# TensorE order written out at three hand-overs of a one-layer trunk: first-token products between transposes, out projection by token halves

## The chip, the cores and the metric

The kernel runs on one core of one Trainium2 chip. The metric is the device time of one execution in microseconds. A core has five engines with an instruction queue each, and each queue runs in order: PE (TensorE, the matrix products), DVE (VectorE), ACT (ScalarE), POOL (GpSimd) and SP (SyncE, which here only starts DMA transfers).

## The reference

One layer over 1024 tokens and 1024 channels, all float32:

```
x = x + 0.5 * (silu(n1 @ w_gate) * (n1 @ w_up)) @ w_down     n1 = rmsnorm(x)        ("f1")
h = rmsnorm(x);  [u v | q k val | gate logits] = h @ w_in                            (mixer)
yA = u * (W_s layernorm(v) + b)       yB = stick-breaking attention, 16 heads of 64
x = x + (sigmoid(gA) * (yA @ W_A) + sigmoid(gB) * (yB @ W_B)) @ W_out
x = x + 0.5 * swiglu(rmsnorm(x))                                                     ("f2")
y = rmsnorm(x)
```

The hidden width of the two feed-forward blocks is 2816.

## The kernel before

**Products.** Every float32 operand is split into a high part (ACT casts it to fp32r) and the rest (a subtraction on DVE or POOL), and one product is three matmuls, high x high, high x low and low x high. Tokens come as eight tiles of 128 (t0 to t7); t0 to t3 are the low half, t4 to t7 the high half.

**A feed-forward block** (`ffn`) multiplies 2x2 block matrices with seven products in place of eight. `right_forms` prepares the token side: for each tile it loads x, takes the sum of squares on ACT (L105), the power -1/2 on POOL (L109), multiplies by the gain on DVE (L123, two halves of 512 channels), transposes eight 128x128 blocks on PE (L204, `nt`) and writes the result by `put` (L208 to L212). A low tile fills the forms B11 and B21, and POOL adds their two parts into `keep` (L218). A high tile makes T2, T1, T3, T4 and B22 from sums with `keep` (L222 to L231); the low parts of T1, T3 and T4 are POOL's. The heart of a high tile is this:

```
tt(t1, n[0], keep[0, t - 4], op=ALU.subtract)
tt(t2, n[1], t1, op=ALU.subtract)
put("T2", t2, tt)
put("T1", t1, pt)
tt(t3, n[1], b12, op=ALU.subtract)
put("T3", t3, pt)
```

Behind the preparation stand the *heads* of the first four weight columns (L269: 24 matmuls of 512 columns each, with B11 and B21, so with low tokens alone), then for each of 22 columns a *tail* (L289: five products with T2, T1, T3, T4 and B22). The down projection ends with a phase called `last` (L398 to L417), in which each finished pair of tiles is written to DRAM, normed and transposed (`after`, `norm_t`, L143) for the mixer.

**The mixer** starts with the value projection `proj_v` (tile `pv`, L67 to L69). It ends with the out projection: `down` takes a fourth of the contraction at a time, for all eight tiles and two column halves: 64 pieces `pd` of six matmuls of 512 columns. In the last fourth each finished tile goes to DRAM (`xres`, L743), and f2 loads it from there (`xr`, L188).

**Order.** Outside of what a program writes by hand, a scheduler with its own timing model orders each engine's queue. In the kernel before it orders everything. It put all 64 transposes of a preparation in front of the heads, and 32 transposes between the last product of f1 and the first of the mixer.

Of the kernel before, what the change touches and what calls it, by code (L numbers as in the profile page):

```python
# [23 lines left out]
XNB = 5  # L24
# [8 lines left out]
class Kernel:  # L33
# [3 lines left out]
    def __init__(self, ctx, tc, a, out):  # L37
        self.tc, self.nc, self.a, self.out, self.ctx = tc, tc.nc, a, out, ctx
        pool = lambda name, bufs, **k: ctx.enter_context(tc.tile_pool(name=name, bufs=bufs, **k))
        self.dram = pool("dram", 1, space=bass.MemoryType.DRAM)  # L40
        self.const = pool("const", 1)
        self.hp = pool("hp", 4)

# [5 lines left out]
    def load_w(self, src, a, b, early=False):  # L49

        nc = self.nc
        raw = self.wp.tile([P, 1024], F32, tag="raw", bufs=2, name="raw")
        nc.sync.dma_start(out=raw.rearrange("p (a b) -> p a b", a=a), in_=src)
        wr = self.wp.tile([P, 2, 1024], F32R, tag="wr", bufs=3, name="wr")
        nc.scalar.copy(wr[:, 0, :], raw)  # L55
        (nc.gpsimd if early else nc.vector).tensor_tensor(wr[:, 1, :], raw, wr[:, 0, :].bitcast(F32), op=ALU.subtract)  # L56
        v = wr.rearrange("p t (a b) -> p t a b", a=a)
        return v[:, 0], v[:, 1]
# [41 lines left out]
    def rstd(self, x2):  # L100
        nc = self.nc
        ss = self.np_.tile([P, 2], F32, tag="ss", name="ss")
        sq = self.psum("p3", "sq")
        for i in range(2):
            nc.scalar.activation(sq, x2[i], AF.Square, accum_out=ss[:, i:i + 1])  # L105
        r = self.np_.tile([P, 2], F32, tag="rs", name="rs")
# [5 lines left out]
    def normed(self, x, gain, tiles, offload):  # L112
# [5 lines left out]
        r = self.rstd(x)  # L118
# [15 lines left out]
    def norm_t(self, x, t, gain, h, offload=1):  # L134

        nc = self.nc
        half, c = t // 4, (t % 4) * P
        xns = [self.np_.tile([P, HALF], F32, tag="xn", bufs=XNB, name="xn") for _ in range(2)]
        self.normed(x[t], gain, xns, offload)
        for i, xn in enumerate(xns):  # L140
            ps = self.psum("p2", "nt")
            for k in range(4):
                nc.tensor.transpose(ps[:, k * P:(k + 1) * P], xn[:, k * P:(k + 1) * P], self.ident)  # L143
            o = [h[half][part][:, i * 4:i * 4 + 4, c:c + P] for part in range(2)]
            self.split(o[0], o[1], ps.rearrange("p (k c) -> p k c", k=4))
# [7 lines left out]
    def form(self, pool, tag, bufs, src):  # L153

        f = pool.tile([P, 2, HALF], F32R, tag=tag, bufs=bufs, name=tag)
        self.split(f[:, 0, :], f[:, 1, :], src)
        return f
# [17 lines left out]
    def right_forms(self, xsrc, gain_src, tp):  # L175


        nc, tt, pt = self.nc, self.nc.vector.tensor_tensor, self.nc.gpsimd.tensor_tensor
        names = ("B11", "B21", "T2", "T1", "T3", "T4", "B22")
        T = {n: (self.hp if i < 4 else tp).tile([P, 4, 2, HALF], F32R, tag="h", name=n) for i, n in enumerate(names)}  # L180
        with self.tc.tile_pool(name="pre", bufs=1, reuse_waits="tile") as pre:
            tmp = lambda tag, bufs: pre.tile([P, HALF], F32, tag=tag, bufs=bufs, name=tag)
            self.np_ = pre
            gain = pre.tile([P, D], F32, tag="gain", name="gain")

            def load(t):
                x = pre.tile([P, D], F32, tag="xr", bufs=2, name="xr")
                nc.sync.dma_start(out=x, in_=xsrc[t * P:(t + 1) * P, :])  # L188
                return x

            keep = {}
            nxt = load(0)
            nc.sync.dma_start(out=gain, in_=gain_src.partition_broadcast(P))
            cut = lambda y: [y[:, i * HALF:(i + 1) * HALF] for i in range(2)]
            r3 = lambda y: y.rearrange("p (k c) -> p k c", k=4)
            for t in range(NT):
                x, nxt = nxt, load(t + 1) if t + 1 < NT else None
                xn = [tmp("xn", 4) for _ in range(2)]
                self.normed(cut(x), cut(gain), xn, 0)
                n = []  # L200
                for i in range(2):
                    ps = self.psum("ps", "nt")
                    for k in range(4):
                        nc.tensor.transpose(ps[:, k * P:(k + 1) * P], xn[i][:, k * P:(k + 1) * P], self.ident)  # L204
                    n.append(ps)
                c = (t % 4) * P

                def put(name, src, sub):  # L208
                    hi, lo = T[name][:, :, 0, c:c + P], T[name][:, :, 1, c:c + P]
                    nc.scalar.copy(hi, r3(src))  # L210
                    sub(lo, r3(src), hi.bitcast(F32), op=ALU.subtract)
                    return hi.bitcast(F32), lo.bitcast(F32)  # L212

                if t < 4:
                    for i, name in enumerate(("B11", "B21")):
                        hi, lo = put(name, n[i], tt)
                        keep[i, t] = tmp("keep", 8)
                        pt(r3(keep[i, t]), hi, lo, op=ALU.add)  # L218
                else:
                    t1, t2, t3, t4 = (tmp("t", 4) for _ in range(4))  # L220
                    b12 = tmp("b12", 1)
                    tt(t1, n[0], keep[0, t - 4], op=ALU.subtract)  # L222
                    nc.scalar.copy(b12, n[0])
                    tt(t2, n[1], t1, op=ALU.subtract)
                    put("T2", t2, tt)
                    put("T1", t1, pt)
                    tt(t3, n[1], b12, op=ALU.subtract)
                    put("T3", t3, pt)
                    put("B22", n[1], tt)
                    tt(t4, t2, keep[1, t - 4], op=ALU.subtract)  # L230
                    put("T4", t4, pt)  # L231
        return T

    def ffn(self, xsrc, gain_src, wg, wu, wd, before, after):

        nc, tc, tt = self.nc, self.tc, self.nc.vector.tensor_tensor
        nff, nj, nhead = DFF // P, DFF // P // 2, 4

# [7 lines left out]
        with ExitStack() as outer:  # L246
# [3 lines left out]
            rawt = lambda: bp.tile([P, D], F32, tag="raw", bufs=4, name="raw")  # L250


            with tc.tile_pool(name="tp", bufs=3, reuse_waits="tile") as tp:
                T = self.right_forms(xsrc, gain_src, tp)
                with tc.tile_pool(name="pa", bufs=1, reuse_waits="tile") as pa:
                    tile = lambda tag, bufs: pa.tile([P, HALF], F32, tag=tag, bufs=bufs, name=tag)

                    def weights(w, f):
                        r = rawt()
                        nc.sync.dma_start(out=r.rearrange("p (k c) -> p k c", k=NK), in_=w[:, f * P:(f + 1) * P].rearrange("(k p) c -> p k c", p=P))  # L260
                        return cut(r)

                    def product(ps, src, right, first, last=True):
                        f = self.form(bp, "wf", 8, src)
                        for k in range(4):
                            ks = slice(k * P, (k + 1) * P)
                            self.mm3f(ps, f[:, 0, ks], f[:, 1, ks], T[right][:, k, 0, :], T[right][:, k, 1, :], first and k == 0, last and k == 3)

                    def head(f):  # L269

                        gate = weights(wg, f)
                        b, a = self.psum("ps", "pb"), self.psum("ps", "pa")
                        product(b, gate[0], "B11", True)
                        p1 = tile("pe", 3)
                        nc.scalar.copy(p1, b)
                        product(a, gate[1], "B21", True)
                        glo = tile("gs", 6)
                        tt(glo, a, p1, op=ALU.add)
                        return gate, b, glo

                    def gated(g, u):

                        s = tile("gs", 6)
# [5 lines left out]
                    def tail(f, gate, b, glo):  # L289
# [18 lines left out]
                        ghi = tile("gs", 6)  # L308
                        tt(ghi, d, w, op=ALU.add)
                        return lo, gated(ghi, uhi)  # L310
# [26 lines left out]
                    heads = {f: head(f) for f in range(nhead)}  # L337
                    for f in range(nff):
                        out = tail(f, *(heads.pop(f) if f in heads else head(f)))
# [7 lines left out]
            with tc.tile_pool(name="pb", bufs=1, reuse_waits="tile") as pb:  # L347
# [11 lines left out]
                def pform(j, src):  # L359
                    return self.form(bp, "wf", 8, src) if j % 2 == 0 else self.form(pb, "pf", 8, src)  # L360
# [36 lines left out]

                def last(js, ts, load=True):  # L398
                    for j in js:
                        if load:  # L400
                            fs[j] = [pform(j, y) for y in pair([dst("a22t4", j)])]
# [3 lines left out]
                last(range(3), range(4))  # L405
                for t in range(4):
                    tt(xh(t + 4, 0), old[t], xh(t + 4, 0), op=ALU.add)
                    tt(xh(t + 4, 1), old[t], xh(t + 4, 1), op=ALU.add)
                after(0, cut(x[0]), cut(gain), 2)
                after(1, cut(x[1]), cut(gain), 2)  # L410
# [366 lines left out]
```

## Time and profile before

| | |
|---|---|
| median of three runs | 2587.96 us (2587.29 to 2589.17) |
| the profiled execution | 2589.35 us, its span 2587.6 us |
| PE busy | 2442.4 us of the span (94%) |
| DVE, ACT, POOL busy | 1715.2, 1048.5, 367.1 us |
| mean granted TensorE clock | 0.975 |

The page of the profile divides the span into 40 slices of 64.7 us and gives each a digit, the busy share in tenths. All DMA of the kernel goes through SP's one queue (313.58 MB). Times in the views are microseconds from the start of the span.

### The profile page before, as it was taken

The numbers are of one execution on the slowest core, as the hardware profiler recorded it, in microseconds if no ns is written. First come the engines' busy times: TensorE is split into PE (matmuls) and PEld (weight loads), VectorE is DVE, ScalarE is ACT, GpSimd is POOL, SyncE is SP. The second block draws the span as 40 slices with busy tenths as digits, with TensorE's granted clock in tenths as the row PEclk, the third lists the DMA queues.
The fourth block names the chain that finished last, engine by engine and source line by source line (L and its number), as shares of the span: only waits on it lengthen the run. The fifth ranks groups of instructions, "written<-read, shape, count | busy, mean of one in ns | idle before, by whom it ended". The sixth has DMA issues, their size and how long they took to land.

```text
span 2587.6 us, 33119 instructions
## 1 busy us (share of the span) xinstructions
PE 2442.4 (94%) x12140; PEld 2069.8 (80%) x12140; DVE 1715.2 (66%) x2617; ACT 1048.5 (41%) x1988; POOL 367.1 (14%) x518
## 2 busy tenths in 40 slices
PE   2999999999999999999999999999929999999998
PEld 2888888788788888888888888888718888887887
DVE  7777777565638878887665555145577777775655
ACT  4333333344536666666422222221043333333535
POOL 4000000000214454444300000000040000000002
PEclk9999999999999999999999999999959999999999
DMA  4345535775421212122111122123243555356754
GB/s 138 116 169 176 171 128 173 250 271 187 139 74 40 58 42 58 42 59 56 34 49 55 46 70 66 55 71 107 87 133 110 171 179 169 129 171 245 263 188 138
DMA packets 250882, 315.69 MB, mean 122 GB/s; under 512 B 14816, under 2 KB 172000, under 8 KB 250720
## 3 DMA queue, kind: packets, MB, share of 16 engines
q1 hardware_dynamic: 250720, 313.58, 37.5%
q8 instruction: 95, 1.56, 0.3%
q14 instruction: 67, 0.55, 0.1%
HBM read 224.93 MB, written 80.22 MB: 118 GB/s over the span
## 4 chain that ended last, share of the span: by engine, by line
PE 58%; DVE 2%; ACT 1%; issue 1%; POOL 1%; DMA 1%; SPq 0%; POOLq 0%; DVEq 0%; ACTq 0%
PE pj L67 6%; PE pj L69 6%; PE pj L68 6%; PE pd L172 4%; PE pd L173 4%; PE pd L171 4%; PE pb L171 2%; PE pb L172 2%; PE pb L173 2%; PE av L532 2%; PE pv L68 2%; PE pv L69 2%; PE pv L67 2%; PE tr L525 2%; PE pa L68 1%; PE pa L67 1%
## 5 line engine op out<-in xcount | busy, mean ns | idle before, releaser
L73 ACT CAST wf<-raw 128x512 fp32r<-128x512 f32 x276 | 164.7, 621 | 301.0 <-PE pd L173 105.0
L74 DVE TENSOR_TENSOR wf<-raw,wf 128x512 fp32r<-128x512 f32 x276 | 183.9, 688 | 142.8 <-ACT wf L73 142.7
L67 PE MATMUL pj<-h,wr 128*128 128x512 f32 x640 | 253.0, 395 | 8.0 <-DVE q L74 8.0
L68 PE MATMUL pj<-h,wr 128*128 128x512 f32 x640 | 251.7, 393 | 0.0
L69 PE MATMUL pj<-h,wr 128*128 128x512 f32 x640 | 251.4, 393 | 0.1
L508 DVE TENSOR_TENSOR_SCAN kp<-kp 128x128 f32<-128x128 f32 (+7 forms) x128 | 181.5, 1423 | 46.5 <-POOL kp L506 45.1
L73 ACT CAST wf<-ws 128x512 fp32r<-128x512 f32 x176 | 108.4, 623 | 195.3 <-PE pd L173 126.6
L56 DVE TENSOR_TENSOR wr<-raw,wr 128x1024 fp32r<-128x1024 f32 x80 | 98.0, 1225 | 82.8 <-ACT wr L55 82.6
L512 POOL TENSOR_TENSOR bt<-bt,kp 128x512 f32<-128x512 f32 (+4 forms) x128 | 132.4, 1035 | 123.3 <-DVE kp L508 97.7
L67 PE MATMUL pv<-wr,h 128*128 128x256 f32 x512 | 146.7, 288 | 1.9 <-ACT vg L574 1.9
L68 PE MATMUL pv<-wr,h 128*128 128x256 f32 x512 | 146.2, 286 | 0.9 <-DVE wr L56 0.9
L67 PEld LDWEIGHTS pj<-h,wr 128*128 128x128 f32 x640 | 121.1, 189 | 32.3 <-DVE q L74 8.6
L69 PE MATMUL pv<-wr,h 128*128 128x256 f32 x512 | 146.2, 286 | 0.0
L69 PEld LDWEIGHTS pj<-h,wr 128*128 128x128 f32 x640 | 121.0, 189 | 25.2 <-DVE wr L56 0.3
L68 PEld LDWEIGHTS pj<-h,wr 128*128 128x128 f32 x640 | 121.0, 189 | 23.6
L55 ACT CAST wr<-raw 128x1024 fp32r<-128x1024 f32 x80 | 84.1, 1052 | 130.9 <-PE pd L69 53.6
L171 PE MATMUL pb<-T,wf 128*128 128x512 f32 x352 | 136.9, 389 | 0.0
L172 PE MATMUL pb<-T,wf 128*128 128x512 f32 x352 | 136.9, 389 | 0.0
L173 PE MATMUL pb<-T,wf 128*128 128x512 f32 x352 | 136.9, 389 | 0.0
L74 DVE TENSOR_TENSOR wf<-ws,wf 128x512 fp32r<-128x512 f32 x176 | 120.0, 687 | 24.7 <-ACT wf L73 24.4
L172 PE MATMUL pd<-wf 128*128 128x512 f32 x336 | 131.4, 391 | 0.0
L173 PE MATMUL pd<-wf 128*128 128x512 f32 x336 | 131.0, 391 | 0.0
(210 smaller groups left out, 6505.7 us busy)
## 6 DMA issues: line engine op xcount, KB each, us to landing
raw<-in_ff_w_down_dram SPq DMA_DIRECT2D x66, 512.0 KB, 6.0
raw<-in_w_in_dram SPq DMA_DIRECT2D x56, 512.0 KB, 3.9
raw<-in_ff_w_gate_dram SPq DMA_DIRECT2D x52, 512.0 KB, 4.3
raw<-in_ff_w_up_dram SPq DMA_DIRECT2D x44, 512.0 KB, 4.7
f_t2t<-as SPq DMA_DIRECT2D x22, 512.0 KB, 4.1
f_a11a<-act SPq DMA_DIRECT2D x44, 256.0 KB, 3.9
f_s2s<-as SPq DMA_DIRECT2D x22, 512.0 KB, 2.8
f_s3s<-as SPq DMA_DIRECT2D x22, 512.0 KB, 5.6
```

The source lines that it names most:

```text
L55: nc.scalar.copy(wr[:, 0, :], raw)
L56: (nc.gpsimd if early else nc.vector).tensor_tensor(wr[:, 1, :], raw, wr[:, 0, :].bitcast(F32), op=ALU.subtract)
L67: mm(ps, lhsT=lh, rhs=rh, start=first, stop=False)
L68: mm(ps, lhsT=lh, rhs=rl, start=False, stop=False)
L69: mm(ps, lhsT=ll, rhs=rh, start=False, stop=last)
L73: self.nc.scalar.copy(hi, src)
L74: self.nc.vector.tensor_tensor(lo, src, hi.bitcast(F32), op=ALU.subtract)
L171: mm(ps, lhsT=lh, rhs=rh, start=first, stop=False, skip_group_check=True)
L172: mm(ps, lhsT=lh, rhs=rl, start=False, stop=False, skip_group_check=True)
L173: mm(ps, lhsT=ll, rhs=rh, start=False, stop=last, skip_group_check=True)
L508: nc.vector.tensor_tensor_scan(rev, rev, rev, 1.0, op0=ALU.mult, op1=ALU.bypass)
L512: eng.tensor_tensor(bt[:, :n], bt[:, :n], kp[:, i * HALF + 1:i * HALF + 1 + n], op=ALU.mult)
```

## The change

**f1's start.** PE and SP get an order by hand there (`manual_schedule`). The heads of columns 0 and 1 are split into halves of 256 tokens: the first halves run when t0 and t1 are there, the second when t2 and t3 are. The heads of columns 2 and 3 run between the transposes of the high tiles. Half of each tile's normalization moves from DVE to POOL (multiply by the gain) and ACT (scale). `keep` is computed in the high tiles instead of the low ones, two additions per tile on POOL; t3 is formed from t2 and `keep`, so that ACT's copy `b12` is gone. The low parts of columns 0's and 1's weights are POOL's too. x has three buffers, not two.

**f1 to the mixer.** PE's order is by hand: the transposes of t0 and t1 stand after the fifth step of the last phase, those of t2 to t5 between the rest of it, those of t6 and t7 between the first `pv` groups. The weight buffers (`raw`, `wf`) are one pool for the whole kernel, so that the loads of w_in need not wait for the end of f1.

**Out projection and f2.** The contraction is run through for the low tokens first, then for the high ones. Each of the eight weight units is loaded and split twice, 16 in all. The low tiles are normed on their way, and their transposes stand between pieces of the high half; B11 and B21 are filled there. f2 is left with t4 to t7, with heads 0 to 3 between their transposes, and loads four tiles of `xres`, not eight.

The core of the diff:

```
-    def right_forms(self, xsrc, gain_src, tp):
...
-                self.normed(cut(x), cut(gain), xn, 0)
...
+    def hi_forms(self, t, xn, T, tmp):
+        tt, pt = self.nc.vector.tensor_tensor, self.nc.gpsimd.tensor_tensor
+        c, keep = (t % 4) * P, []
+        for name in ("B11", "B21"):
+            keep.append(tmp("keep", 2))
+            hi, lo = (T[name][:, :, part, c:c + P].bitcast(F32) for part in range(2))
+            pt(keep[-1].rearrange("p (k c) -> p k c", k=4), hi, lo, op=ALU.add)
+        n = self.transposed(xn)
+        t1, t2, t3, t4 = (tmp("t", 4) for _ in range(4))
+        tt(t1, n[0], keep[0], op=ALU.subtract)
+        tt(t2, n[1], t1, op=ALU.subtract)
+        self.put(T["T2"], t, t2, tt)
+        self.put(T["T1"], t, t1, pt)
+        tt(t3, t2, keep[0], op=ALU.subtract)
+        self.put(T["T3"], t, t3, pt)
+        self.put(T["B22"], t, n[1], tt)
+        tt(t4, t2, keep[1], op=ALU.subtract)
+        self.put(T["T4"], t, t4, pt)
...
+                def head_part(h, cs=slice(0, HALF)):
+                    first = cs.start == 0
+                    h[3] = h[3] or self.psum("ps", "pa")
+                    passes(h[2], h[1][0], "B11", first, True, cs)
+                    passes(h[3], h[1][1], "B21", first, True, cs)
...
+                    def norm(t):
+                        xn = [tmp("xn", 4) for _ in range(2)]
+                        self.normed(cut(x[t]), cut(gain), xn, 1)
+                        return xn
...
+                    if ready:
+                        heads[0], heads[1] = head(0), head(1)
...
+                        work = {4: 0, 5: 1, 6: 2, 7: 3}
+                    else:
...
+                        heads[1] = head(1, pool)
+                        self.lo_forms(0, norm(0), T)
+                        self.lo_forms(1, norm(1), T)
+                        head_part(heads[0], q[0])
+                        load(4)
+                        self.lo_forms(2, norm(2), T)
+                        head_part(heads[1], q[0])
...
+                        work = {5: 2, 6: 3}
+                    for t in range(4, NT):
+                        xn = norm(t)
+                        if t in work:
+                            f = work[t]
...
+                            head_part(heads[f])
+                            full(f)
...
+                        self.hi_forms(t, xn, T, tmp)
...
+                    for t in range(4):
+                        last(range(6, nj), [t], t == 0)
+                        tt(xh(t + 4, 0), xh(t + 4, 0), A[t], op=ALU.subtract)
+                        lo.append(after(t + 4, cut(x[t + 4]), cut(gain), 1))
+                        f = lo.pop(0)
+                        f and f()
+                self.pending = [f for f in lo if f]
...
+                if quad == 0 and t and self.pending:
+                    self.pending.pop(0)()
...
+                if t < 4:
+                    xn[t] = [self.utile("xn") for _ in range(2)]
+                    self.normed(x[t], gain, xn[t], 1)
...
+                for half in range(2):
+                    for c0 in range(0, NK, FCH):
+                        wds = [self.load_cols(a["w_out"][0], i * HALF, c0, FCH, HALF) for i in range(2)]
+                        ts = range(4 * half, 4 * half + 4)
+                        act = [m[c0 + k, half] for k in range(FCH)]
+                        if c0 + FCH < NK:
+                            for i in range(2):
+                                for n, t in enumerate(ts):
+                                    self.piece(x, act, wds, t, i, ("p0", "p1"))
+                                    if half == 1 and c0 == 0 and n % 2:
+                                        self.lo_forms(2 * i + n // 2, xn[2 * i + n // 2], T)
```

PE's queue at f1's start, before (B_93 is B11; `pb` and `pa` are the two banks of a head):

```order
L773 UNCONDITIONAL_BRANCH
L204 MATMUL nt<-ident,xn 128x128 x64
L171 MATMUL pb<-B_93,wf 128x512
L172 MATMUL pb<-B_93,wf 128x512
L173 MATMUL pb<-B_93,wf 128x512
```

The same place after, cut to the first rows of each run of products (B_99 is B11, B_100 is B21):

```order
L182 MATMUL nt<-ident,xn 128x128 x16
L171 MATMUL pb<-B_99,wf 128x256
...
L171 MATMUL pa<-B_100,wf 128x256
...
L182 MATMUL nt<-ident,xn 128x128 x8
L171 MATMUL pb<-B_99,wf 128x256
...
L182 MATMUL nt<-ident,xn 128x128 x8
...
L171 MATMUL pb<-B_99,wf 128x512
...
L182 MATMUL nt<-ident,xn 128x128 x8
```

The 64 transposes are split up into two tiles, one, one, one, one and two, with the products of heads 0 to 3 between them.

POOL's queue in two high tiles of f1's preparation, before (T_96, T_97, T_98 are T1, T3 and T4):

```order
L211 TENSOR_TENSOR T_96<-t,T_96 128x4x128
L109 TENSOR_TENSOR rs<-rs,neghalf 128x1
L211 TENSOR_TENSOR T_97<-t,T_97 128x4x128
L211 TENSOR_TENSOR T_98<-t,T_98 128x4x128
L211 TENSOR_TENSOR T_96<-t,T_96 128x4x128
L109 TENSOR_TENSOR rs<-rs,neghalf 128x1
L211 TENSOR_TENSOR T_97<-t,T_97 128x4x128
L211 TENSOR_TENSOR T_98<-t,T_98 128x4x128
```

and after (T_102, T_103, T_104 are T1, T3 and T4; the piece is of t5 and t6):

```order
L116 TENSOR_TENSOR xn<-xr,gain 128x512
L191 TENSOR_TENSOR T_102<-t,T_102 128x4x128
L108 TENSOR_TENSOR rs<-rs,neghalf 128x1
L206 TENSOR_TENSOR keep<-B_99 128x512
L191 TENSOR_TENSOR T_103<-t,T_103 128x4x128
L206 TENSOR_TENSOR keep<-B_100 128x512
L191 TENSOR_TENSOR T_104<-t,T_104 128x4x128
L191 TENSOR_TENSOR T_102<-t,T_102 128x4x128
```

A high tile had three subtractions and one power on POOL; it now has two additions of `keep` and a multiplication of 128x512 as well.

SP's queue between the out projection and f2's preparation, after:

```order
L257 DMA raw<-in_ff_w_gate_dram 128x8x128 x2
L814 DMA xres<-x 128x512 x8
L306 DMA gain<-in_ff_norm_dram 128x1024
L294 DMA xr<-xres 128x1024 x4
L257 DMA raw<-in_ff_w_gate_dram 128x8x128 x3
```

Only t4 to t7 are written and read back here. The first read stands behind all eight writes of the high tiles.

## Rows read from the trace of the kernel before

**Rows 1.** The page, lines of part 2: PE and its granted clock, 40 slices.

```profile
PE   2999999999999999999999999999929999999998
PEclk9999999999999999999999999999959999999999
```

**Rows 2.** Windows: stretch, length, each engine's busy time (instructions), clock, DMA share.

```profile
0.00:63.26 63.26, 15.95 (x64) 12.17 (x65) 45.79 (x68) 30.74 (x68) 29.44 (x31) 1.00 0.47 141
63.26:87.14 23.88, 23.88 (x99) 19.58 (x97) 19.00 (x27) 9.54 (x17) 4.58 (x3) 1.00 0.47 132
87.14:141.70 54.56, 54.56 (x242) 45.20 (x241) 41.05 (x67) 21.42 (x36) 0.00 (x0) 1.00 0.46 147
705.40:719.93 14.53, 5.75 (x32) 4.53 (x31) 12.66 (x18) 10.90 (x21) 3.53 (x4) 0.63 0.53 157
1785.90:1873.30 87.40, 86.24 (x380) 70.75 (x378) 50.63 (x72) 5.90 (x7) 0.00 (x0) 1.00 0.25 91
1873.30:1941.20 67.90, 16.05 (x65) 12.29 (x65) 47.31 (x67) 30.01 (x67) 27.87 (x25) 0.52 0.43 136
1941.20:1965.10 23.90, 23.90 (x100) 19.63 (x99) 19.26 (x28) 9.58 (x18) 4.59 (x3) 0.92 0.46 134
```

**Rows 3.** Timeline, PE, f1's start: start, time, instruction [idle before <-releaser].

```profile
36.41 1.94 PE L204 MATMUL nt<-ident,xn 128*128 128x128 f32 x8 [4.27 <-DVE xn L123]
```

**Rows 4.** Timeline, DVE, f1's start.

```profile
23.17 1.41 DVE L123 SCALAR_TENSOR_TENSOR xn<-xr,rs,gain 128x512 f32<-128x512 f32 x2 [1.95 <-POOL rs L109]
...
45.95 0.68 DVE L222 TENSOR_TENSOR t<-nt,keep 128x512 f32<-128x512 f32 x1
...
50.84 3.36 DVE L123 SCALAR_TENSOR_TENSOR xn<-xr,rs,gain 128x512 f32<-128x512 f32 x2
54.12 0.68 DVE L222 TENSOR_TENSOR t<-nt,keep 128x512 f32<-128x512 f32 x1
```

**Rows 5.** Timeline, POOL, f1's start.

```profile
20.14 2.49 POOL L218 TENSOR_TENSOR keep<-B 128x512 f32<-128x512 f32 x2 [4.33 <-DVE B L211]
...
47.84 1.27 POOL L211 TENSOR_TENSOR T<-t,T 128x512 fp32r<-128x512 f32 x1 [2.36 <-ACT T L210]
49.87 0.87 POOL L109 TENSOR_TENSOR rs<-rs,neghalf 128x1 f32<-128x1 f32 x1 [0.75 <-DVE rs L108]
50.70 2.95 POOL L211 TENSOR_TENSOR T<-t,T 128x512 fp32r<-128x512 f32 x2
...
64.25 4.71 POOL L211 TENSOR_TENSOR T<-t,T 128x512 fp32r<-128x512 f32 x3 [2.42 <-ACT T L210]
```

**Rows 6.** Groups of POOL by line between 671.3 and 720: count, busy, mean ns.

```profile
L117 POOL TENSOR_TENSOR xn<-x,gain 128x512 f32<-128x512 f32 x11 | 14.3, 1319 | 119.3 <-DVE x L395 117.9 <-PE nt L143 1.4
```

**Rows 7.** Timeline, PE, f1 to the mixer.

```profile
705.22 1.03 PE L143 MATMUL nt<-ident,xn 128*128 128x128 f32 x8
...
712.37 1.97 PE L143 MATMUL nt<-ident,xn 128*128 128x128 f32 x8 [4.02 <-DVE xn L123]
```

**Rows 8.** Timeline, ACT, f1 to the mixer.

```profile
709.52 2.00 ACT L55 CAST wr<-raw 128x1024 fp32r<-128x1024 f32 x2
```

**Rows 9.** Timeline, PE, out projection to f2.

```profile
1872.04 0.39 PE L69 MATMUL pd<-wr,ml 128*128 128x512 f32 x1
1889.46 1.94 PE L204 MATMUL nt<-ident,xn 128*128 128x128 f32 x8 [17.03 <-DVE xn L123]
```

**Rows 10.** Timeline, SP's DMA queue, out projection to f2.

```profile
1879.23 1.57 SPq L188 DMA_DIRECT2D xr<-xres  x1
```

**Rows 11.** Timeline, ACT, out projection to f2.

```profile
1885.84 0.60 ACT L105 ACTIVATE sq<-xr 128x512 f32<-128x512 f32 x1 [1.98 <-DMA xr<-xres]
```

**Rows 12.** Instructions on tile raw between 1740 and 1874: duration ns, start, landing.

```profile
L55 ACT CAST wr<-raw x10: 1053/1053/1056, 1741.4 to 1844.7; 128x1024 fp32r<-128x1024 f32 x10
L56 DVE TENSOR_TENSOR wr<-raw,wr x10: 1215/1216/1225, 1742.7 to 1845.8; 128x1024 fp32r<-128x1024 f32 x10
...
DMA to landing us min/median/max: 3.3/3.4/6.0
```

More of the change, by code (lines that the diff above doesn't have):

```diff
@@ L42, in __init__ @@
         self.hp = pool("hp", 4)
+        self.wp = pool("wp", 1, reuse_waits="tile")
     def mixer_psum(self, tag, name):
@@ L173, in mm3f @@
         mm(ps, lhsT=ll, rhs=rh, start=False, stop=last, skip_group_check=True)
-    def right_forms(self, xsrc, gain_src, tp):
[L178 to L198, printed above, removed]
-                self.normed(cut(x), cut(gain), xn, 0)
[L200 to L232, printed above, removed]
@@ L234, in ffn, with transposed, put @@
-    def ffn(self, xsrc, gain_src, wg, wu, wd, before, after):
+    def transposed(self, xn):
+        ps = []
+        for i in range(2):
+            p = self.psum("p2", "nt")
+            for k in range(4):
+                self.nc.tensor.transpose(p[:, k * P:(k + 1) * P], xn[i][:, k * P:(k + 1) * P], self.ident)
+            ps.append(p)
+        return ps
+    def put(self, form, t, src, sub):
+        c = (t % 4) * P
+        hi, lo = form[:, :, 0, c:c + P], form[:, :, 1, c:c + P]
+        r3 = src.rearrange("p (k c) -> p k c", k=4)
+        self.nc.scalar.copy(hi, r3)
+        sub(lo, r3, hi.bitcast(F32), op=ALU.subtract)
@@ new lines, in first_forms, with lo_forms @@
+    def first_forms(self):
+        return {n: self.hp.tile([P, 4, 2, HALF], F32R, tag="h", name=n) for n in ("B11", "B21")}
+    def lo_forms(self, t, xn, T):
+        for name, n in zip(("B11", "B21"), self.transposed(xn)):
+            self.put(T[name], t, n, self.nc.vector.tensor_tensor)
+    def hi_forms(self, t, xn, T, tmp):
[16 more added lines that the diff above has]
+        self.put(T["T4"], t, t4, pt)
@@ L236, in ffn @@
+    def ffn(self, xsrc, gain_src, wg, wu, wd, before, after, T=None):
         nc, tc, tt = self.nc, self.tc, self.nc.vector.tensor_tensor
         nff, nj, nhead = DFF // P, DFF // P // 2, 4
+        ready = T is not None
         scratch = {n: self.dram.tile([nj * P, D], F32, name=f"{self.stage}_{n}") for n in ("a11a12", "s2s1", "s3s4", "a22t4", "t2t1", "t3")}
@@ L255, in ffn @@
                 with tc.tile_pool(name="pa", bufs=1, reuse_waits="tile") as pa:
                     tile = lambda tag, bufs: pa.tile([P, HALF], F32, tag=tag, bufs=bufs, name=tag)
[L258 to L279, printed above, removed]
@@ L281, in gated @@
                     def gated(g, u):
[L283 removed]
+                        s = tile("gs", 2)
                         nc.scalar.activation(s, g, AF.Sigmoid)
@@ L335, in right_sums @@
                             nc.sync.dma_start(out=dst(n, j, i), in_=y)
-                    heads = {f: head(f) for f in range(nhead)}
                     for f in range(nff):
-                        out = tail(f, *(heads.pop(f) if f in heads else head(f)))
+                        if f not in heads:
+                            heads[f] = head(f)
+                            head_part(heads[f])
+                            full(f)
+                        out = tail(f, *heads.pop(f))
                         if f % 2 == 0:
@@ L400, in last @@
                         if load:
-                            fs[j] = [pform(j, y) for y in pair([dst("a22t4", j)])]
+                            fs[j] = [late((j - 6) * 2 + i, y) if j >= 6 else wform(y) for i, y in enumerate(pair([dst("a22t4", j)]))]
                         for t in ts:
                             step(*fs[j], A[t], t, j == 0, j == nj - 1)
[L405 to L408, printed above, removed]
@@ new lines, in ffn @@
+                with tc.manual_schedule(engines={mybir.EngineType.PE}):
+                    lo = []
+                    last(range(3), range(4))
+                    for t in range(4):
+                        tt(xh(t + 4, 0), old[t], xh(t + 4, 0), op=ALU.add)
+                        tt(xh(t + 4, 1), old[t], xh(t + 4, 1), op=ALU.add)
+                    for t in (0, 1):
+                        lo.append(after(t, cut(x[t]), cut(gain), 2))
+                    last(range(3, 5), range(4))
+                    for f in lo:
+                        f and f()
+                    lo = [after(t, cut(x[t]), cut(gain), 2) for t in (2, 3)]
+                    last(range(5, 6), range(4))
+                    for t in range(4):
+                        last(range(6, nj), [t], t == 0)
+                        tt(xh(t + 4, 0), xh(t + 4, 0), A[t], op=ALU.subtract)
+                        lo.append(after(t + 4, cut(x[t + 4]), cut(gain), 1))
+                        f = lo.pop(0)
+                        f and f()
@@ L442, in attention, with piece @@
+                self.pending = [f for f in lo if f]
+    def piece(self, x, act, wds, t, i, tags):
+        c = (t % 4) * P
+        ps = self.psum(tags[t % 2], "pd")
+        for k in range(FCH):
+            ah, al = act[k]
+            self.mm3(ps, ah[:, c:c + P], al[:, c:c + P], wds[i][0][:, k, :], wds[i][1][:, k, :], k == 0, k == FCH - 1)
+        self.nc.vector.tensor_tensor(x[t][i], ps, x[t][i], op=ALU.add)
     def attention(self, ap, ydram):
```

171 lines of the change are left out of this document (103 added, 68 removed).

## The prediction, made before the changed kernel ran

> **What bounds the kernel now.** I read the page first. PE is busy in 94% of the span, and its row of 40 digits is 9 nearly everywhere, with a 2 in the first slice and a 2 in the slice near 1900; the granted clock falls to 5 in that one as well [rows 1]. So the end is set by PE, and outside of these places only PE's own work could shorten it. The windows then give the idle time of each place. From 0 to 63.26 PE is busy for 15.95 us while DVE is busy for 45.79: this is f1's preparation. From 705.40 to 719.93 it is 5.75 of 14.53, at a clock of 0.63: f1 to the mixer. From 1873.30 to 1941.20 it is 16.05 of 67.90, at 0.52: the out projection to f2 [rows 2]. The stretches behind the preparations, 23.88 and 23.90 us long, hold heads without a gap, and the tails behind f1's are full too [rows 2]. That the heads stand behind the last transposes is a matter of order: they use low tokens only. The timelines show what makes a preparation slow. From one high tile to the next DVE takes 54.12 - 45.95 = 8.17 us, with little idle [rows 4], and four such periods from t4's transposes at 36.41 [rows 3] give 69.1, where T4 of t7 is in fact done at 64.25 + 4.71 = 68.96 [rows 5].
>
> **The first term: f1's start.** Before, the tails start at 87.14 [rows 2]. After, no head is left behind the last high tile, and PE's queue has T2 (2 matmuls), T1 (2) and then T4's product, which waits for POOL. A head matmul takes 86.24/380 = 0.227 us at full clock [rows 2], so this is 0.9 us behind T4's last low part.
>
> When is that done? I leave t4's transposes at 36.4: a low tile gets half a multiplication shorter, but 24 or 48 products of 256 columns come between. In a high tile DVE now multiplies one half, not two: 3.36 for two [rows 4] becomes 0.7 to 1.7, and the DVE chain of 8.17 falls to about 6.2. POOL gets more. It had 1.27 + 0.87 + 2.95 = 5.09 busy and 2.36 + 0.75 = 3.11 idle in a tile [rows 5]; two additions of `keep` cost 2.49 [rows 5] and the multiplication 1.32 [rows 6], 3.81 together. So POOL becomes the bound at 5.09 + 3.81 = 8.9 us per tile, if DVE's work fits beside it. T4 of t7 is then done at 36.4 + 4 x 8.9 = 72.0, the tails start at 72.9, and 14.2 us are won. Two costs come off. After idle time PE starts at a low clock: the heads took 23.88 where 96 x 0.227 = 21.8 are needed, 2.1 more [rows 2], and the tails will pay this in their place. And the first tail's weight forms, which DVE and ACT made beside the heads, may come late: I take 1. The term is 11 us, between 3 (POOL and DVE strictly in turn, see below) and 18 (the period stays at 8.17 and no cost).
>
> At this place the Trainium skill speaks against the change. The row: two multiplications on DVE take 1.41 alone and 3.36 beside two POOL subtractions [rows 4, 5]. The page "SBUF — State Buffer", section "Who interferes with whom", says that an instruction on DVE with two SBUF inputs contends with a POOL instruction that reads SBUF, and that the pair of ports they share is an exclusive lock. The trace agrees, since 3.36 is about 1.41 and most of POOL's 2.95 [rows 5]. By the rule the sum would be that of the first rival below, by the rows without it that of the forecast.
>
> **The second term: f1 to the mixer.** Of 14.53 us, 8.78 are idle, and the 32 transposes take 5.75 where four times 1.03 would do at full clock [rows 2, 7]: 1.6 more. The transposes themselves stay. In the changed order those of t2 to t5 stand between steps of `last`, of which each leaves PE some 7 us of work, and those of t6 and t7 behind groups of the value projection. So nearly all of 8.78 + 1.6 = 10.4 can go. What is late next is the weights: the casts of w_in are done at 709.52 + 2.00 = 711.5, DVE's part 1.2 later [rows 8, 12]; if they came as they do now, the value projection could not start before 712.7, and 7.2 us would be won. Their loads no longer wait for f1's buffers, so I take 10, between 5 and 12.
>
> **The third term: out projection to f2.** Before, from the last piece (1872.04 + 0.39) to the first tail (1941.20 + 23.9 = 1965.1) there are 92.7 us [rows 2, 9]. After:
> - the transposes of t0 to t3 stand between pieces and cost PE their own 4 x 1.03 = 4.1 at full clock [rows 7];
> - SP issues the first read of `xres` at 1879.23, 6.8 after the last piece, behind eight tiles' writes and weight loads [rows 10]. In the new queue it stands behind the last write only, so I put it 0.5 after the last piece, and 6.8 is the other end. From issue to the first square it is 1885.84 - 1879.23 = 6.6 [rows 10, 11], from there to the transposes 1889.46 - 1885.84 = 3.6 [rows 9, 11]: t4's transposes come 10.7 after the last piece instead of 17.03;
> - four high tiles at 8.9 are 35.6, the two first products 0.9;
> - clock and forms as in f1's start, 3.
>
> The sum is 4.1 + 10.7 + 35.6 + 0.9 + 3 = 54.3, and 92.7 - 54.3 = 38 us are won. The bounds are 27 (alternating, 2.8 a tile) and 45 (8.17 a tile, no clock cost).
>
> **Edits at nothing.** Eight more weight units cost ACT 8 x 1.05 and DVE 8 x 1.22 us, and 8 loads of 3.4 [rows 12]. DVE is busy for 50.63 of 87.40 there and ACT for 5.90 [rows 2]; each unit serves four pieces, 24 x 0.227 = 5.4 us, and three units are in rotation. A unit needs 3.4 + 1.05 + 1.22 = 5.7 from load to use, so two units of lead hide it; what it costs without the lead is the third rival. The norms of t0 to t3 lie beside pieces as well. Reordered queues in the attention I put at 0, plus or minus 3.
>
> **The sum.** 11 + 10 + 38 = 59. The profiled execution took 2589.35 us, 2587.6 of it span; its time less 59 is 2530.3. It lies 1.4 above the median of the runs, so I say 2530.
>
> **The rivals.**
> 1. *POOL and DVE strictly in turn.* If each of DVE's four operations with two inputs in SBUF (the multiplication, T2's low part, t3 and t4, 0.7 each) waits while POOL works, a high tile takes 8.9 + 2.8 = 11.7. That costs 4 x 2.8 = 11.2 us at each of two preparations: 2552. For it: 3.36 against 1.41 [rows 4]. Against it: POOL still had gaps while the waits of the row went on [rows 5]. The section of the Trainium skill named above would give this.
> 2. *Low clock beside the heads.* Transposes took 1.94 for eight at low clock and 1.03 at full [rows 7, 9]; a head of 24 products is 5.4 or 10.3. With transposes a tile would be 12.2 on PE, 3.3 over the 8.9, for two heads in f1 and three in f2: 17 us, 2547. For it: 0.52 granted in f2's preparation [rows 2]. Against it: PE is to be busy twice as long there.
> 3. *The other side: the weights of the out projection are not hidden.* If the unit is loaded only when a buffer is released by the pieces before it, all 5.7 us show: 16 x 5.7 = 91 against 59 won, 2589 - 59 + 91 = 2621, slower. It decides from 59/16 = 3.7 us shown per unit. Against it: before, eight units in the same rotation left 87.40 - 86.24 = 1.2 us idle in all [rows 2].
> 4. *The change does less than it says.* The forms of the first tails were made under the heads: DVE was busy for 19.00 and 19.26 us there, and is busy for 41.05 of 54.56 in the tails, so it has little to spare [rows 2]. If all that work now stood behind T4, 38 us would go back: 2568. Against it: DVE has about 2.7 us per high tile free.
> 5. *POOL does not bind.* If the additions of `keep` fit into its gaps and DVE's shorter chain sets the pace, a tile takes 7.4: 4 x 1.5 = 6 us more at each preparation, 2518. For it: 3.11 us of gaps per tile [rows 5].
>
> **How the numbers follow.** Forecast 0.48 (2530, with a range of 2516 to 2546), rival 1 0.12 (2552), rival 2 0.13 (2547), rival 3 0.05 (2621), rival 4 0.05 (2568), rival 5 0.17 (2518). The range from 2505 to 2560 leaves out rivals 3 and 4 and the far ends of the others. A change under 0.2% (5 us) is not told from none. Faster takes all but rival 3 and a sliver of cases in which several go wrong together: 0.93; same 0.02, slower 0.05.
>
> **What would show it.** The first tail product in f1 near 73 us instead of 87, with POOL's T4 row as its releaser; POOL busy almost without a gap from t4 to t7, with a period near 8.9; no PE idle over 2 us between the last `pd` of f1 and the value projection; t4's transposes in f2 about 11 us after the last piece and the first tail about 50 after it; PE idle under 5 us in the out projection. I am wrong if PE waits for weights in the out projection, if heads are cut by a low clock in the high tiles, or if PE waits for DVE's forms in the first tails.

## The result: 2552.5 us, 35.5 faster, where 59 were forecast

The changed kernel takes 2552.49 us (median of four runs, 2550.41 to 2553.66) against 2588.02 before: a ratio of 0.9861, 95% interval 0.9844 to 0.9879. The sign is as forecast and the time lies in the range from 2505 to 2560, but above the 2516 to 2546 that the prediction gave its own mechanism. The profiled execution took 2552.09 us, its span 2550.3; against the span before it is 37.3 us shorter, so of the 59 us of the sum 22 are missing.

To see where they are missing I read the start time of the same instruction in both traces at five marks. The lead is how much earlier it comes than before.

| mark | before, us | lead of the changed kernel | its step | forecast |
|---|---|---|---|---|
| f1's last tail product | 488.68 | 9.06 | +9.1 | +11 |
| first product of the attention (`z`) | 766.15 | 8.51 | -0.6 | +10 |
| last product of the out projection | 1872.04 | 3.97 | -4.5 | -4.1 |
| f2's last tail product | 2366.29 | 42.44 | +38.5 | +42 |
| end of the span | 2587.6 | 37.3 | -5.1 | 0 |

The 4.1 in the third line are the transposes of t0 to t3, which the third term had counted: 34 were won by it, not 38. The second hand-over won nothing, and the end, in which nothing was forecast, lost 5.

### The profile page after: what moved, and what is told of

Same layout as the page of the kernel before. It is cut to its first block, busy times and chain, and to the rows that moved or that the text cites. A ratio compares the mean times of both kernels' runs of the same rounds, so it can differ in the third digit from the quotient of the medians.

```text
span 2550.3 us, 33259 instructions
## 1 busy us (share of the span) xinstructions
PE 2429.8 (95%) x12188; PEld 2060.4 (81%) x12188; DVE 1716.0 (67%) x2605; ACT 1054.4 (41%) x2004; POOL 391.5 (15%) x538
## 4 chain that ended last, share of the span: by engine, by line
PE 85%; DVE 5%; DMA 4%; issue 1%; ACT 1%; SPq 0%; POOL 0%; POOLq 0%; DVEq 0%; ACTq 0%
PE pj L67 7%; PE pj L68 7%; PE pj L69 7%; PE pd L171 7%; PE pd L172 7%; PE pd L173 7%; PE pb L171 4%; PE pb L172 4%; PE pb L173 4%; PE av L598 3%; PE tr L591 2%; PE pv L67 2%; PE pv L69 2%; PE pv L68 2%; PE pe L171 2%; PE pe L172 2%
## 5 line engine op out<-in xcount | busy, mean ns | idle before, releaser
L156 DVE TENSOR_TENSOR wf<-raw,wf 128x512 fp32r<-128x512 f32 x276 | 192.0, 717 | 121.3 <-ACT wf L155 121.2
L67 PE MATMUL pj<-h,wf 128*128 128x512 f32 x640 | 253.7, 396 | 5.3 <-DVE q L74 5.3
L68 PE MATMUL pj<-h,wf 128*128 128x512 f32 x640 | 252.9, 395 | 0.0
L69 PE MATMUL pj<-h,wf 128*128 128x512 f32 x640 | 252.2, 395 | 0.0
L574 DVE TENSOR_TENSOR_SCAN kp<-kp 128x128 f32<-128x128 f32 (+7 forms) x128 | 181.1, 1421 | 39.9 <-POOL kp L572 38.5
L57 DVE TENSOR_TENSOR wf<-raw,wf 128x1024 fp32r<-128x1024 f32 x88 | 108.3, 1231 | 143.8 <-ACT wf L56 143.3
L56 ACT CAST wf<-raw 128x1024 fp32r<-128x1024 f32 x88 | 92.8, 1055 | 219.0 <-PE pj L68 116.7
L116 POOL TENSOR_TENSOR xn<-x,gain 128x512 f32<-128x512 f32 x16 | 23.0, 1463 | 883.4 <-DVE x L450 469.3
L67 PE MATMUL pv<-wf,h 128*128 128x256 f32 x512 | 145.2, 286 | 2.1 <-ACT vg L641 2.1
L67 PEld LDWEIGHTS pj<-h,wf 128*128 128x128 f32 x640 | 121.9, 190 | 30.0 <-DVE q L74 6.0
L69 PE MATMUL pv<-wf,h 128*128 128x256 f32 x512 | 145.3, 284 | 0.0
L68 PE MATMUL pv<-wf,h 128*128 128x256 f32 x512 | 145.1, 284 | 0.0
L69 PEld LDWEIGHTS pj<-h,wf 128*128 128x128 f32 x640 | 121.6, 190 | 25.1 <-DVE wf L57 0.2
L68 PEld LDWEIGHTS pj<-h,wf 128*128 128x128 f32 x640 | 121.7, 190 | 24.1
```

The lines of the kernel that those rows point to most:

```text
L56: nc.scalar.copy(hi, raw)
L57: (nc.gpsimd if early else nc.vector).tensor_tensor(lo, raw, hi.bitcast(F32), op=ALU.subtract)
L67: mm(ps, lhsT=lh, rhs=rh, start=first, stop=False)
L68: mm(ps, lhsT=lh, rhs=rl, start=False, stop=False)
L69: mm(ps, lhsT=ll, rhs=rh, start=False, stop=last)
L156: (sub or self.nc.vector.tensor_tensor)(f[:, 1, :], src, f[:, 0, :].bitcast(F32), op=ALU.subtract)
```

## The profile after

PE and its clock by slices; the first slice, 2 before, is now 5, and the two of the out projection to f2 are 7 and 8 [rows 1]:

```profile
PE   5899999999899999999999999999978999999998
PEclk9899999999999999999999999999999999999999
```

Windows of the changed kernel with the columns of [rows 2]: f1's start, f1's end to the mixer, the out projection, and from its end to the first tail:

```profile
0.00:75.77 75.77, 33.90 (x209) 29.48 (x209) 53.05 (x73) 42.36 (x86) 51.93 (x46) 0.86 0.42 122
...
686.65:711.00 24.35, 15.93 (x79) 13.47 (x78) 15.26 (x28) 15.82 (x35) 5.62 (x7) 0.79 0.36 113
1782.00:1868.50 86.50, 85.54 (x388) 69.32 (x386) 66.47 (x99) 27.23 (x44) 7.71 (x8) 1.00 0.40 132
1868.50:1920.97 52.47, 27.80 (x129) 22.58 (x129) 42.36 (x53) 25.43 (x52) 39.12 (x28) 0.81 0.42 126
```

POOL is busy for 51.93 of 75.77 us. From 41.87 on it has no gap, and T4 of t7 is done at 65.99 + 6.72 = 72.71 (72.0 forecast, 68.96 before [rows 5]). Its timeline:

```profile
51.74 1.71 POOL L191 TENSOR_TENSOR T<-t,T 128x512 fp32r<-128x512 f32 x1
53.42 0.99 POOL L108 TENSOR_TENSOR rs<-rs,neghalf 128x1 f32<-128x1 f32 x1
...
65.99 6.72 POOL L191 TENSOR_TENSOR T<-t,T 128x512 fp32r<-128x512 f32 x4
```

PE in f1's start, f1 to the mixer and f2's start; the brackets hold the idle time and its releaser, as in [rows 3, 7, 9]:

```profile
75.77 0.80 PE L171 MATMUL pb<-T,wf 128*128 128x512 f32 x1 [17.50 <-ACT wf L155]
...
695.24 1.97 PE L182 MATMUL nt<-ident,xn 128*128 128x128 f32 x8 [8.42 <-ACT xn L120]
...
1880.40 1.97 PE L182 MATMUL nt<-ident,xn 128*128 128x128 f32 x8 [5.35 <-DVE xn L122]
...
1920.97 0.79 PE L171 MATMUL pb<-T,wf 128*128 128x512 f32 x1 [16.70 <-ACT wf L155]
```

The first tail comes 3.1 us behind T4 and is released by its weight form, not by POOL. At 695.24 stands what the second term had overlooked: the 8.8 us of waits that were behind the last product of f1 are now one wait of 8.42 inside `last`, for t2. ACT, DVE and POOL show its origin (ACT: squares L104, weights' casts L56, scale L120; POOL: multiplications L116):

```profile
686.67 0.60 ACT L104 ACTIVATE sq<-x 128x512 f32<-128x512 f32 x1 [1.72 <-DVE h L74]
...
692.15 1.04 ACT L56 CAST wf<-raw 128x1024 fp32r<-128x1024 f32 x1 [1.65 <-DMA raw<-in_w_in_dram]
...
694.48 2.55 ACT L120 ACTIVATE xn<-xn,rs 128x512 f32<-128x512 f32 x4
```

```profile
679.04 5.79 DVE L156 TENSOR_TENSOR pf<-raw,pf 128x512 fp32r<-128x512 f32 x4 [0.97 <-ACT pf L155]
...
685.96 1.27 DVE L74 TENSOR_TENSOR h<-nt,h 128x512 fp32r<-128x512 f32 x2
```

```profile
679.12 5.15 POOL L116 TENSOR_TENSOR xn<-x,gain 128x512 f32<-128x512 f32 x3 [3.90 <-DMA raw<-f_a22t]
```

t2's squares write to a PSUM bank (`sq`) which DVE releases only when it has read t0's transposes from it (L74), and DVE gets to that late: four subtractions took 5.79 us beside POOL's multiplications. Then t2's scale stands in ACT's queue behind a cast that waits for the weights.

## The experiments

All are edits of the changed kernel (2552.49 us), timed against the kernel before. The table holds their medians and, from the one execution of each that was profiled, the leads at the five marks. That execution can lie some us from the median: in 3 it took 2539.90 us where the median is 2544.20.

| kernel | us | f1 tails | `z` | out proj. | f2 tails | end |
|---|---|---|---|---|---|---|
| changed | 2552.49 | 9.06 | 8.51 | 3.97 | 42.44 | 37.3 |
| 1 last free, both | 2545.26 | 9.09 | 14.44 | 7.64 | 46.53 | 44.2 |
| 2 last free, f2 | 2549.99 | 9.19 | 9.26 | 1.95 | 40.31 | 39.8 |
| 3 squares in SBUF | 2544.20 | 10.52 | 19.53 | 13.35 | 52.53 | 49.4 |
| 4 T3 on DVE | 2550.69 | 10.05 | 10.22 | 5.42 | 44.07 | 38.9 |
| 5 t2 in PSUM | 2542.54 | 15.30 | 15.25 | 11.54 | 52.73 | 47.5 |
| 6 sums later | 2551.66 | 11.14 | 9.27 | 4.01 | 41.97 | 36.7 |
| 7 out, all tokens | 2571.17 | 10.20 | 10.73 | 9.51 | 22.52 | 19.3 |
| 8 heads behind | 2554.32 | 13.08 | 11.06 | 5.76 | 43.96 | 35.2 |
| 9 three mends | 2531.24 | 15.32 | 22.88 | 18.92 | 60.20 | 59.7 |
| 10 mult. on DVE | 2553.06 | 9.48 | 9.28 | 2.62 | 40.57 | 35.7 |
| 11 heads later | 2528.65 | 18.08 | 27.66 | 20.85 | 60.22 | 58.8 |
| 12 two x buffers | 2553.43 | 11.30 | 10.16 | 4.79 | 43.69 | 35.5 |

**1 and 2, the order of the last phase.**

```
-                with tc.manual_schedule(engines={mybir.EngineType.PE}):    # around last
+                with ExitStack():                                          # 1
+                with ExitStack() if ready else tc.manual_schedule(...):    # 2: f2 alone
```

1: 

> PE's order by hand is taken away in the last phase of both feed-forward blocks; all else is as in the changed kernel (2552.5 us). Theory: the hand-over from f1 to the mixer won nothing (the first z product came 8.5 us earlier than before, exactly the lead that f1's first product of the down projection already had), because PE waits 8.4 us for t2's scaled tile in the new order; and the same order cost f2's end 4.6 us. Then the time is about 2548 (between 2545 and 2555). Rival: the order is worth the 10 us that I predicted and the loss came from elsewhere: 2560 to 2563.

2: 

> PE's order by hand is taken away in the last phase of f2 only. Theory: the stretch from f2's first down product to the end goes from 236.0 us back to the 231.4 of the kernel before, the time is 2548. Rival: the 4.6 us come from something else in that stretch (the loads, the weight buffers shared by all stages): the stretch stays at 236 and the time at 2552.

1: ratio 0.9829 (0.9815 to 0.9844). From f1's tails to `z` the scheduler's order wins 5.4 us and the written one loses 0.6, so that the written order is 6 us worse here: more than the theory said, and against the rival. 2: from f2's first down product to the end it takes 231.1 us, 231.2 before and 235.7 in the changed kernel; from its last tail product 221.8, 221.3 and 226.4. The order cost the end 4.6 us, as expected; 2549.99 (0.9849, 0.9833 to 0.9865) shows only 2.5 of it, since in this kernel 2.8 more were lost between `z` and the out projection. The other rows of the table agree: with the written order in f2's last phase 3.1 to 8.8 us are lost between f2's tails and the end, with the scheduler's (1, 2, 9, 11) 0.5 to 2.3.

**3, the bank of the squares.**

```
-        r = self.rstd(x, self.psum("p3", "sq") if offload == 2 else tiles[0])
+        r = self.rstd(x, self.np_.tile([P, HALF], mybir.dt.bfloat16, tag="sq", ...) if offload == 2 else tiles[0])
```

> Where the norm of a low tile is taken from DVE (f1's and f2's last phase), ACT's squares go to an SBUF tile (bfloat16, never read) instead of a PSUM bank. Theory: t2's squares waited for the bank that t0's transposes held, and PE's wait of 8.4 us for t2 is this wait and what stands behind it; PE's wait there falls under 3 us and the time to about 2545. Rival: the wait is that of DVE's and ACT's queues behind POOL's multiplications (four subtractions took 5.8 us instead of 2.5) and of the weights' casts: it stays above 6 us and the time within 2 us of 2552.5.

2544.20 (0.9826, 0.9811 to 0.9841), as expected. PE in the last phase, transposes of t2 to t5: no wait over 0.84 is left, and the hand-over wins 9.0 us. The four subtractions beside POOL's multiplications still take 5.80 us, so that the rival's queues do not make the wait without the bank.

```profile
684.28 1.04 PE L182 MATMUL nt<-ident,xn 128*128 128x128 f32 x8
688.62 1.04 PE L182 MATMUL nt<-ident,xn 128*128 128x128 f32 x8
693.95 1.09 PE L182 MATMUL nt<-ident,xn 128*128 128x128 f32 x8 [0.84 <-DVE xn L122]
698.32 1.03 PE L182 MATMUL nt<-ident,xn 128*128 128x128 f32 x8
```

**4, 5 and 10, what sets the pace of the high tiles.**

```
-        self.put(T["T3"], t, t3, pt)                     # 4
+        self.put(T["T3"], t, t3, tt)
-        t1, t2, t3, t4 = (tmp("t", 4) for _ in range(4)) # 5
+        t1, t3, t4 = (tmp("t", 4) for _ in range(3))
+        t2 = self.psum("p2", "t2")
-                        self.normed(cut(x[t]), cut(gain), xn, 1)   # 10
+                        self.normed(cut(x[t]), cut(gain), xn, 0)
```

4: 

> In the high tiles the low part of T3 is DVE's work, not POOL's, at both preparations. Theory: POOL sets the pace there (in f1 it was busy without a gap from 41.87 to 72.71), so taking away 1.3 to 1.7 us per tile brings T4 of t7 4 to 6 us earlier at each preparation: about 2542 (2540 to 2546). Rival: DVE's operations with two SBUF inputs and POOL's take turns, so the same work on DVE costs 0.7 instead of 1.3 per tile and only 2.4 us per preparation are won: 2547 to 2549. Third: DVE becomes the bound, no gain: 2551 to 2554.

5: 

> In the high tiles t2 is written to a PSUM bank, not to SBUF, so three of DVE's four operations with two inputs in SBUF (t3, t4, T2's low part) have one only; no operation is added or moved. Theory: DVE and POOL take turns on operations that read two tiles from SBUF; from 41.87 to 72.71 in f1 POOL's own work is 25.2 us (12 subtractions, 6 additions, a multiplication at 1.27, two powers at 0.55) and 5.6 us are waiting. Then T4 of t7 is done about 5 us earlier at each preparation, and the time is 2542 to 2545. Rival: the pace is set by the chain through PE, DVE and ACT from tile to tile; T4 of t7 moves by less than 2 us and the time stays within 2551 to 2554.

10: 

> The preparation's multiplication by the gain goes back to DVE for both halves (no multiplication on POOL, no scale on ACT); otherwise the changed kernel. Theory of DVE and POOL in turn: POOL's 1.27 is replaced by DVE's 0.7, so T4 of t7 comes no later than 72.7 in f1 and the time is 2548 to 2553. Rival: it was DVE's chain from tile to tile that the change cut (3.36 us for two multiplications), and the high tiles go back to over 8 us each: T4 of t7 at 75 or later, 2556 or more.

4 (0.9853, 0.9838 to 0.9868): one operation per tile less on POOL won 1.0 us at f1's tails and 0.7 at f2's first tail. T4 of t7 came 1.5 us earlier, at 71.18, and POOL had gaps again. My theory that POOL's amount of work sets the pace fell; the time lies between the rival's range and the third case, nearer to the third. 5 (0.9821, 0.9806 to 0.9836) takes no work away, only the second SBUF input of three DVE operations, and T4 of t7 is done at 60.96 + 7.06 = 68.02 instead of 72.71, 4.7 us earlier (5 expected). POOL's rows show why, though its operations are the same: `keep` takes 2.49 and 2.94 for two and five subtractions 7.06, so that fewer of them are stretched to 1.7.

```profile
51.93 2.94 POOL L206 TENSOR_TENSOR keep<-B 128x512 f32<-128x512 f32 x2
...
58.51 2.49 POOL L206 TENSOR_TENSOR keep<-B 128x512 f32<-128x512 f32 x2
60.96 7.06 POOL L191 TENSOR_TENSOR T<-t,T 128x512 fp32r<-128x512 f32 x5
```

10 (0.9865, 0.9848 to 0.9881): with the multiplication back on DVE T4 comes at 66.34 + 6.73 = 73.07 and the time is the same. The theory of turns misses its range by 0.4 us of T4 and 0.06 of the time; the rival's 75 and 2556 are farther off.

**6, the sums of w_down.** `right_sums(0)` is issued with the second tail instead of the first.

> The sums of w_down for the first pair of columns (four DVE operations, which stand ahead of the first tail's weight forms) are issued with the second tail, in both blocks. Theory: the 3.1 us between T4 of t7 and the first tail product are the first tail's own weight sums behind these operations; about 2 us are won at each preparation, 2548. Rival: what is won at the tail's start is paid later, since DVE has the same work: 2551 to 2554.

2551.66 (0.9851, 0.9834 to 0.9867). f1's first tail comes 1.05 us earlier, f2's stands 51.3 behind the last piece instead of 52.9, and nothing is left at the end: the rival's case.

**7, the third hand-over undone.** The old loop over all tokens with eight weight loads; f2 starts like f1 (`T=None`).

> The third hand-over is undone: the out projection runs over all eight tiles with eight weight loads, and f2 prepares eight tiles with f1's new order. Theory: then f2's first tail comes 17 us (the transposes of t0 after the last piece, as before) plus 65.2 (from there to the tail, as in f1 of the changed kernel) after the last piece, 82 instead of 52.5 + 4.1 for the moved transposes: 25 us slower than the changed kernel, 2578. Rival: the third hand-over is worth what I predicted for it in full, 38 us, and f1's order gives nothing here: 2590. Other rival: the doubled weight loads cost what the halves win, and the time is under 2565.

2571.17 (0.9931, 0.9916 to 0.9946): 18.7 us slower than the changed kernel, 7 less than expected. From the last piece to the first tail it takes 77.2 us (82 expected). So f1's new preparation alone brings f2's tails 13 us forward, and the token halves the rest of the third term.

**8 and 12, the heads and the x buffers in f1.** 8 issues all four heads after `hi_forms` of t7; 12 is 8 with two buffers for x.

8: 

> In f1's start the four heads stand behind all transposes, as before the change; all other edits stay (POOL's multiplication, keep, three buffers for x). Theory: the order is what won time there: the heads start near 60 and the first tail near 84 instead of 75.8, PE starts cold in the heads and not in the tails, and the time is 2557 to 2561. Rival: the products between the transposes slow the high tiles, so that without them the preparation ends earlier and most of it comes back: 2551 to 2555.

12: 

> The kernel with f1's heads behind all transposes (2554.3 us), with two buffers for x in f1's preparation instead of three. Theory: before the change, the tiles came at the pace of the loads of x, since a load waited until the buffer's tile was multiplied (ACT's squares waited 11.6 us for x in all); the third buffer is what made f1's preparation shorter, not the order of the heads. Then t4's transposes come at 35 to 36 instead of 29.0, the first tail 5 to 7 us later (80 to 82 instead of 74.6), and the time is 2559 to 2562. Rival: the moved multiplication, or keep's move out of the low tiles, shortened it: the first tail stays within 2 us of 74.6, the time within 2 us of 2554.3.

Both theories fell, and both times lie in the rivals' ranges. 8 (0.9866, 0.9851 to 0.9881) has its first tail at 74.63, before the changed kernel's 75.77, and its last one 4 us before; 2.5 of these 4 us are gone by f2's tails, and a slower end (8.8 us lost behind f2's tails) takes the rest; why the end is slower there stays open. PE's transposes of t6 and t7 in it, and POOL's last operations:

```profile
46.77 1.94 PE L182 MATMUL nt<-ident,xn 128*128 128x128 f32 x8 [12.43 <-DVE xn L122]
50.64 1.94 PE L182 MATMUL nt<-ident,xn 128*128 128x128 f32 x8 [1.93 <-DVE xn L122]
```

```profile
59.20 6.95 POOL L191 TENSOR_TENSOR T<-t,T 128x512 fp32r<-128x512 f32 x4
```

Before, t7's transposes came in two halves at 60.84 and 62.53, so that they now start some 10 us earlier. T4 of t7 is done at 66.15: 6.6 us before the changed kernel's 72.71, as the rival said, but only 2.8 before the 68.96 of [rows 5]. The tails do not wait for it; they stand behind the heads, which run from 52.23 to the first tail. So the two orders come out alike: with the heads in front PE waits 17.50 for the first tail, with the heads behind it works up to it. What the heads in front cost is seen in the changed kernel: the scaled tiles of t4 and t5 were there at 28.13 and 31.60, and their transposes came at 34.51 and 42.21, behind products of the heads. 12 (0.9872, 0.9855 to 0.9889) has t4's transposes at 28.84 with two buffers, so the third one is not the reason. By 10 it isn't the multiplication alone either: there t4's transposes come at 33.09. What is left is `keep`, which no longer stands in the low tiles, the heads' weight forms on POOL, and SP's order, which has x ahead of the weights. I didn't separate these.

**9 and 11, versions that beat both.** 9 joins 3, 5 and 2. 11 is 9 with t4's transposes ahead of the second halves of heads 0 and 1, t5's ahead of head 2, t6's ahead of head 3.

9: 

> The changed kernel with three of the edits above together: squares in SBUF, t2 in PSUM, f2's last phase in the scheduler's order. Theory: they mend different places, so their gains add: about 10 at the hand-over to the mixer, 5 and 5 at the preparations, 3 to 5 at the end: 2528 to 2534, what I had predicted for the change. Rival: the places share their slack (a lead won early is lost in the mixer or at the end) and only half of it arrives: 2536 to 2541.

11: 

> The kernel with three mends, and in f1's start t4's transposes stand ahead of the second halves of heads 0 and 1, t5's ahead of head 2 and t6's ahead of head 3. Theory: with the heads in front, the transposes of t4 waited for 96 products of 256 columns and the high tiles began 5 to 6 us later than with the heads behind (POOL's first T subtraction at 41.9 instead of 36.9), so T4 of t7 comes at about 63 and the first tail at 65 to 66 instead of 70.5: 4 to 5 us faster than the kernel with three mends. Rival: POOL and DVE are busy from the low tiles on, T4 of t7 moves by less than 2 us, and the time with it.

9: 2531.24 (0.9781, 0.9766 to 0.9796). The gains add: 22.4 us of lead at the end over the changed kernel. 11: 2528.65 (0.9771, 0.9756 to 0.9785), the lowest median; T4 of t7 at 57.88 + 7.06 = 64.94 and the first tail at 67.4 instead of 70.5, so 3 us earlier and not the 4 to 5 expected. f1's last tail comes 2.8 earlier than in 9, but at f2's tails nothing of that lead is left (60.22 against 60.20), and the intervals overlap: that 11 is faster than 9 isn't shown.

## Why the prediction was right in sign and too large in size

That the time lies in the range is in part luck: 2552 is the time of rival 1, but most of what brought it there, t2's wait and the loss at the end, stood in no term and in no rival.

**f1's start, 11 forecast, 9.1 found.** The place of T4, 72.0, was right to 0.7 us, by two errors that nearly cancel: t4's transposes came at 34.51 and not at 36.4, and from there to T4 it took 38.2, 9.55 per tile and not 8.9. POOL was gapless as said, but the pace was not its 8.9 us of work; it was DVE and POOL in turn (4 against 5). And the step "no head is left behind the last high tile" was not what won the time: with the heads behind, the tails end 4 us earlier (8). The rows showed a preparation of 63 us and I kept its low tiles at 36.4; they became shorter, and the heads in front of t4's transposes used most of that up. The 1 us that I took for the first tail's forms was 3.1 - 0.9 = 2.2; that PE waits for them was one of the signs of being wrong that the prediction named. The 2.1 taken off for a low clock came as 2.3: the granted clock was 0.67 from 75 to 85, where the tails began, and 1.00 in the first 10 us of the tails before, and they took 403.9 us instead of 401.5.

**f1 to the mixer, 10 forecast, -0.6 found.** This step failed, and it is half of what is missing. It said that each part of `last` between the transposes leaves PE 7 us of work, so that nearly all waits go. A part is 15 products of 0.227, 3.4 us, and the rows of the changed kernel have the transposes 4.3 apart. Above all I asked when PE would be ready and not when t2's tile would be: its squares need a PSUM bank that t0 holds. The bank mended, the hand-over wins 9.0 (3), and the term was right as a size.

**Out projection to f2, 38 forecast, 34 found.** The transposes of t4 came 11.9 us after the last piece (10.7 forecast), T4 37.5 behind them (35.6), the tail 3.1 later (0.9). The weights cost nothing: PE waited 0.9 us in all in the out projection, for DVE's reading of the transposes' banks, so rival 3 is refuted. Rival 2 is right in that transposes waited for heads, but not in the clock: in f2's start t5's and t6's scaled tiles were there at 1881.54 and 1891.85, and their transposes came 6.9 and 3.0 us later, behind a head. But the granted clock was 0.81 there, the head between t4 and t5 took 6.4 us and not 10.3, and a tile took 37.5/4 = 9.4 us and not 12.2.

**The end, 0 forecast, -5.1 found.** I had not seen that the written order of `last` holds in f2 as well (2).

**Rival 1** had the time that came, 2552, and half its mechanism: DVE and POOL did take turns (5), but what 5 gives back of that is 6.2 us at f1's tails and 2.7 at f2's (5 against the changed kernel), not 11.2 at each; the rest of what was missing was the wait for t2 and the end. Rival 5 is refuted by POOL's gapless rows, rival 4 but for the 2.2 us of the first tails' forms. The Trainium skill says in "SBUF — State Buffer", section "Who interferes with whom", that a DVE instruction with two SBUF inputs contends with a POOL instruction that reads SBUF, and that one with at most one SBUF input, outside the modes that use both ports, does not. The trace and 5 bear it out: an operation of DVE with one SBUF input ran at 0.68 beside POOL, one with two took up to 1.78.

## What to carry to other kernels

Where an order is written out by hand, work out for each instruction that is moved forward when its operands and its buffers are free, scratch banks included: the wait moves with it. Leave the hand order off every stage that merely shares the code. And when two engines take turns on a resource, changing where an operand lies can win more than moving work from one to the other.

## What the runs showed of the hardware that I had not expected

DVE's and POOL's waits for each other look like work in the busy time: POOL's subtraction of 128x512 took 1.27 alone and 1.71 beside DVE, DVE's multiplication 0.75 and, beside two of POOL's subtractions, 1.78:

```profile
47.20 1.78 DVE L122 SCALAR_TENSOR_TENSOR xn<-xr,rs,gain 128x512 f32<-128x512 f32 x1 [0.15 <-POOL rs L108]
```

POOL's gapless 30.8 us held, by an estimate from 1.27 for each of its 128x512 operations and 0.55 for a power, some 25 us of its own work, which no busy share shows.
